# The experts' loop of a hybrid decoder layer: a pair's scatter placed among the next pair's first products, and both experts' first products ahead of the second ones

## The chip, the core and the metric

The kernel runs on one core of a Trainium2 chip. A core has TensorE (PE: matrix products; its weight loads are listed as PEld), VectorE (DVE), ScalarE (ACT), GpSimd (POOL) and SyncE (SP), which here issues the transfers. TensorE's clock has two levels, 1.2 and 2.4 GHz; the profile gives the granted clock as a share of the higher one. The metric is the device time of one execution in microseconds (us), as the median of several runs.

## The reference

One decoder layer is computed for 256 tokens of width 2048: a norm with modulation, a mixer, a residual addition, a second norm, a mixture of experts, a residual addition and a final norm. All values are float32. Only the mixture matters here: each token goes to 2 of 32 experts, and each expert is a gated product of width 512.

```python
def expert_block(args):                       # one expert e, a block of rows xb
    xb, e = args
    hid = jax.nn.silu(xb @ w_gate[e]) * (xb @ w_up[e])     # 2048 -> 512, twice
    return hid @ w_down[e]                                 # 512 -> 2048
...
y = grouped_expert_mlp(xt, eidx, w_gate, w_up, w_down)     # (T, 2, D)
return jnp.einsum('tk,tkd->td', gates.astype(y.dtype), y).reshape(B, S, D)
```

The weights of one expert are 8 + 4 MiB, so the 32 experts bring 384 MiB that are each read once.

## The kernel before

The mixer's part ends at about 680 us; what follows is the experts' loop (`for e in range(0, NE, 2)`), which takes the experts in 16 pairs. Four experts' tokens are gathered at once (`Slots.gather_all`, tiles `xg`, in PSUM bank `g`), so a gather stands at every second pair. For an expert, up to 64 tokens fill the slots.

- `hidden` makes the **first products** (tile `u`, line 1136 and the next): 8 ring tiles of 1 MiB, each with gate and up weights for 256 rows of the input. ScalarE and VectorE then make `hid` (L1140, L1141), TensorE transposes it (L1144, bank `t`), VectorE copies it to `hidT` (L1146).
- `seconds` makes the **second products** (tile `d`): 4 ring tiles of 1 MiB. VectorE scales the result into `z` (L1165), ScalarE rounds it to `yah` or `ybh` (L1168), VectorE forms the rest `yal` or `ybl` (L1169).
- `scatter` brings a finished pair back to the tokens: 8 **blocks** of four products each (`yah`, `yal`, `ybh`, `ybl` with the one-hot matrix `wt`), all of them in the single PSUM bank `s`, each followed by VectorE's addition to the residual tile `xt` (L1182). A block can begin only when the addition of the block before has read the bank.
- `back` makes `wt` and the gates `gs` of a pair, through bank `t` (products `t<-identr,oh` and `t<-Ge,oh`). `further` counts overfull experts, in the first pair only.

All weights go through one ring of slots, 14 of 1 MiB in this loop, which `Stream` hands out in the order of the code: a load is added for each tile (`exp_load`, issued on SP at L191), and it gets the slot of the tile that was used 14 tiles earlier. SP's queue runs in order: a load whose slot is not free yet holds up all loads behind it.

The order within an engine's queue is not that of the code. A scheduler with a timeline of its own sorts the instructions when the kernel is built; waits for slots, banks and tiles decide at run time. L65 is the helper `mm` that records every product. TensorE's products in float32 leave two records each in the trace, so that a ring tile is 8 records of `u` or 16 of `d`.

Of the kernel before, what the change touches and what calls it, by code (L numbers as in the profile page):

```python
# [8 lines left out]
F32 = mybir.dt.float32  # L9
F32R = mybir.dt.float32r  # L10
# [3 lines left out]
ALU = mybir.AluOpType  # L14
AX = mybir.AxisListType

P = 128
D = 2048
NB = 2
KT = 16  # L20
# [9 lines left out]
NE = 32  # L30
# [18 lines left out]
def hybrid_moe(ctx: ExitStack, tc: tile.TileContext, x, c, norm1_g, norm2_g, early, ada_w, ada_b, w_bb,  # L49
# [3 lines left out]
    V, S, G, T = nc.vector, nc.scalar, nc.gpsimd, nc.tensor  # L53
# [10 lines left out]
    def mm(o, lhsT, rhs, start=True, stop=True):  # L64
        return T.matmul(o, lhsT, rhs, start=start, stop=stop, skip_group_check=True)  # L65
# [20 lines left out]
    x1 = x_tiles()  # L86
# [16 lines left out]
    def bank(tag, bufs=None, name=None):  # L103
        return psum.tile([P, 512], F32, name=name or tag, tag=tag, bufs=bufs or BANKS[tag])
# [56 lines left out]
    st = Stream()  # L161
# [28 lines left out]
    def exp_load(w, e, j):  # L190
        return lambda t: nc.sync.dma_start(t, w[e, j])  # L191
# [279 lines left out]
    w_items = [(early_load("out", n, q), None) for qs in ((0, 3), (1, 2)) for n in range(4) for q in qs]  # L471
    for s, load, _ in a_cols + c_cols + z_cols + on(st, w_items) + rows_q:
        s.add(load)
    for e in range(NE):
        for j in range(KT // 2):
            st.add(exp_load(expert_gu, e, j))
        for n in range(4 if e < NE - 2 else 0):
            st.add(exp_load(expert_dn, e, n))

    for n in range(4):  # L480
        for e in (NE - 2, NE - 1):
# [537 lines left out]
    def hid_tile(name):  # L1019
        return cst.tile([P, 4, 4, 40], F32, name=name, tag="rw").rearrange("p n k e -> p (n k e)")[:, 0:512]  # L1020
# [105 lines left out]
                       self.ge[:, b, 2 * a:2 * a + 2], start=(b == 0), stop=(b == 1))  # L1126
            V.tensor_copy(self.gs.rearrange("p h u -> p (h u)"), p[:, 0:4])

    def hidden(u, us, xg, st):
        us = slice(SL * us, SL * (us + 1))  # L1130
        p = bank("u", 2)
        for j in range(KT // 2):
            t = st.get().rearrange("p (k w n) -> p k w n", k=2, w=2)
            for k in range(2):
                kt = 2 * j + k
                mm(p[0:64], xg[:, kt, us], t[:, k, 0], start=(kt == 0), stop=(kt == 15))
                mm(p[64:128], xg[:, kt, us], t[:, k, 1], start=(kt == 0), stop=(kt == 15))
            st.done()
        hid = hid_tile("hid")
        S.activation(hid[64:128], p[0:64], AF.Silu)  # L1140
        V.tensor_tensor(hid[0:64], hid[64:128], p[64:128], op=ALU.mult)  # L1141
        p = bank("t", 1)
        for ft in range(4):
            T.transpose(p[:, SL * ft:SL * (ft + 1)], hid[0:64, P * ft:P * (ft + 1)], ident[0:64, 0:64])  # L1144
        hT = hidT[:, u]
        V.tensor_copy(hT.rearrange("p f s -> p (f s)"), p[:, 0:256])  # L1146
        return hT
# [23 lines left out]
    def seconds(u, hT, gs, ys, st, yl=None):  # L1171
        for n in (0, 2):
            second(u, hT, gs, ys, st, n, 2, yl)

    def scatter(n, wt, yh, yl):
        c = slice(256 * n, 256 * (n + 1))
        for b in range(NB):
            p = bank("s", 1)
            for h in range(2):
                mm(p[:, 256 * h:256 * (h + 1)], wt[:, h, b], yh[h][:, c], start=True, stop=False)  # L1180
                mm(p[:, 256 * h:256 * (h + 1)], wt[:, h, b], yl[h][:, c], start=False, stop=True)
            V.tensor_tensor(x1[n][:, b], x1[n][:, b], p, op=ALU.add)  # L1182

    def scatter_late(n, wt, ys):
        for h, y in enumerate(ys):
            p = bank("g", 2)
            for b in range(NB):
                mm(p[:, 256 * b:256 * (b + 1)], wt[:, h, b].bitcast(F32), y[:, 256 * n:256 * (n + 1)])
            xh = x1[n][:, :, 256 * h:256 * (h + 1)]
            V.tensor_tensor(xh, xh, p.rearrange("p (b j) -> p b j", b=NB), op=ALU.add)  # L1190
# [12 lines left out]
    def new_y(dt, s):  # L1203
        return tuple(mp.tile([P, 1024], dt, name=f"y{h}{s}", tag=f"y{h}{s}", bufs=1) for h in "ab")
# [6 lines left out]
    def further():  # L1211
# [11 lines left out]
        V.tensor_copy(ovi, ove[:, NE - 1:NE])  # L1223
        V.memset(kc, 0.0)

    for e in range(0, NE, 2):
        a = e // 2 % 2
        if not a:
            sl = Slots(Pm[:, :, e:e + 4], Ge[:, :, e:e + 4], 2)
            sl.gather_all()  # L1230
        if e:
            sl.back(a)
        if e == NE - 2:
            hT = [hidden(u, 2 * a + u, sl.xg, st) for u in range(2)]
            break
        hT = hidden(0, 2 * a, sl.xg, st)
        if not e:
            gates()
            sl.back(a)
            further()  # L1240
        yh, yl = new_y(F32R, "h"), new_y(F32R, "l")
        seconds(0, hT, sl.gs, yh, st, yl)
        seconds(1, hidden(1, 2 * a + 1, sl.xg, st), sl.gs, yh, st, yl)
        for n in range(4):
            scatter(n, sl.wt, yh, yl)

    def spare_tile(name, shape):
        pool, tag = slot = next(x for x in st.free if x[0] is not ring1)
# [10 lines left out]
    ys = new_y(F32, "h")  # L1259
    for n in range(4):  # L1260
        for u in range(2):
            second(u, hT[u], sl.gs, ys, st, n, 1)
        scatter_late(n, sl.wt, ys)
        squares(n)
        if n == 0:
            scaled()
            S.activation(small("warm", [P, 1]), ss3[:, 0, 0:1], AF.Sqrt)
# [6 lines left out]
    with tc.For_i(0, nov, 1):  # L1274
        V.tensor_scalar(osel, ovs, kc, None, op0=ALU.is_le)
        V.scalar_tensor_tensor(osel, ove, kc, osel, op0=ALU.is_gt, op1=ALU.mult)
        V.tensor_scalar(oacc, ovs, kc, -float(SL), op0=ALU.subtract, op1=ALU.mult)
        V.scalar_tensor_tensor(oacc, oacc, float(SL), osel, op0=ALU.add, op1=ALU.mult, accum_out=oev[:, 0:1])
        V.scalar_tensor_tensor(oacc, iota32, 0.0, osel, op0=ALU.add, op1=ALU.mult, accum_out=oev[:, 1:2])
        V.tensor_copy(oei, oev[:, 1:2])  # L1280
        ev = nc.sync.value_load(oei[0:1, 0:1], min_val=0, max_val=NE - 1)
        for b in range(NB):
            V.scalar_tensor_tensor(oacc, Pm[:, b], 0.0, osel, op0=ALU.add, op1=ALU.mult, accum_out=opm[:, b, 0:1])
            V.scalar_tensor_tensor(oacc, Ge[:, b], 0.0, osel, op0=ALU.add, op1=ALU.mult, accum_out=opm[:, b, 1:2])
            V.tensor_scalar(opm[:, b, 0:1], opm[:, b, 0:1], oev[:, 0:1], None, op0=ALU.subtract)
        V.tensor_scalar(kc, kc, 1.0, None, op0=ALU.add)
        so = Stream()
        es = bass.ds(ev, 1)

        def dyn(w, j):  # L1290
            return lambda t: nc.sync.dma_start(t, w[es, j].rearrange("e p n -> p (e n)"))

        for w, m in ((expert_gu, KT // 2), (expert_dn, 4)):
            for j in range(m):
                so.add(dyn(w, j))
        so.grow(*main, *side)
        sl = Slots(*(opm[:, :, i:i + 1].to_broadcast([P, NB, 2]) for i in range(2)), 1)
        sl.gather_all()
        sl.back(0)
        ys = new_y(F32, "h")  # L1300
        G.memset(ys[0][64:128], 0.0)
        G.memset(ys[1][0:64], 0.0)
        seconds(0, hidden(0, 0, sl.xg, so), sl.gs, ys, so)
        for n in range(4):
            scatter_late(n, sl.wt, ys)
            squares(n)
        scaled()
# [80 lines left out]
```

## Time and profile before

| | |
|---|---|
| median of 3 runs | 1670.57 us (1669.73 to 1675.09) |
| profiled execution, its own time | 1678.59 us |
| its span, first to last instruction | 1676.8 us |
| mean granted clock of TensorE | 0.962 |
| busy share of the span | PE 93%, DVE 40%, ACT 24%, POOL 11% |
| moved in all | 573.77 MB, 342 GB/s over the span |
| SP's transfers | 85.0% of 16 DMA engines' span |

The profiled execution has a time of its own, above the median, and the durations below are parts of it. A busy share says how much of the span an engine had an instruction in progress, not that it ran at full speed.

### The profile page before, as it was taken

To read this page: it belongs to the slowest core of one execution; us is meant where nothing else is said; L and a number is where in the kernel's file an instruction comes from. 1 tells how busy PE (TensorE), PEld (TensorE's weight loads), DVE (VectorE), ACT (ScalarE), POOL (GpSimd) and SP (SyncE) were. 2 spreads that over 40 slices of the span, in tenths; PEclk is the share of its full clock that TensorE was granted. 3 is DMA by queue.
4 is the path that set the end of the run, shared out by engine and by line. 5 is a ranking of instruction groups with operands and counts; after the bars stand their busy time and mean duration, and the time that the engine had idled before them with its cause. 6 is when DMAs were issued, how large, how long until landed. Compare 5 with 4: busy or idle time off the path is not lost. (4 is left out here: it accounts for less than half of the span.)

```text
span 1676.8 us, 23825 instructions
## 1 busy us (share of the span) xinstructions
PE 1558.4 (93%) x10064; PEld 962.1 (57%) x10064; DVE 670.5 (40%) x1138; ACT 400.8 (24%) x685; POOL 182.5 (11%) x104
## 2 busy tenths in 40 slices
PE   5899899999999999889989889989999999999995
PEld 3678767888877677445444444444444545445443
DVE  3534755234424444343332333333433433434324
ACT  3323654344246344021010011011011011111102
POOL 1111222452223231000000000000000000000000
PEclk8999999999999999899989898999999999999998
DMA  9985467545598784799899798989999999999996
GB/s 391 402 321 225 161 222 282 224 172 203 190 330 334 299 357 160 256 422 420 355 400 421 308 422 353 422 361 420 421 421 421 421 420 420 421 421 420 421 421 231
DMA packets 82438, 573.77 MB, mean 342 GB/s; under 512 B 9740, under 2 KB 10100, under 8 KB 13336
## 3 DMA queue, kind: packets, MB, share of 16 engines
q1 hardware_dynamic: 82080, 572.02, 85.0%
q8 instruction: 81, 1.33, 0.3%
q14 instruction: 29, 0.24, 0.0%
q10 hardware_dynamic: 248, 0.19, 0.0%
HBM read 570.07 MB, written 2.10 MB: 341 GB/s over the span
## 5 line engine op out<-in xcount | busy, mean ns | idle before, releaser
L65 PE MATMUL u<-ring,xg 128*64 128x512 f32 x2048 | 475.6, 599 | 0.0
L65 PEld LDWEIGHTS u<-ring,xg 128*64 128x64 f32 x2048 | 139.8, 137 | 240.0 <-issue 220.1
L65 PE MATMUL d<-ring,hidT 128*64 128x256 f32 x2048 | 250.4, 401 | 9.6 <-DVE hidT L1146 9.6
L65 PE MATMUL w<-hx,stg 128*128 128x256 f32 x1392 | 198.3, 294 | 9.8 <-ACT stg L289 3.1
L65 PEld LDWEIGHTS d<-ring,hidT 128*64 128x64 f32 x2048 | 148.8, 144 | 93.2 <-issue 16.7
L65 PEld LDWEIGHTS w<-hx,stg 128*128 128x128 f32 x1392 | 177.5, 195 | 41.5 <-issue 24.0
L290 POOL TENSOR_TENSOR stg<-ring,stg 128x1024 fp32r<-128x1024 f32 x53 | 128.1, 2417 | 412.4 <-ACT stg L289 370.2
L1182 DVE TENSOR_TENSOR xt<-xt,s 128x512 f32<-128x512 f32 x120 | 82.4, 687 | 225.0 <-PE s L65 224.2
L289 ACT CAST stg<-ring 128x1024 fp32r<-128x1024 f32 x116 | 121.2, 1047 | 187.8 <-PE w L65 150.8
L1165 DVE SCALAR_TENSOR_TENSOR z<-d,gs,g2b 64x512 f32<-64x512 f32 x120 | 90.0, 750 | 166.2 <-PE d L65 164.2
L290 DVE TENSOR_TENSOR stg<-ring,stg 128x1024 fp32r<-128x1024 f32 x63 | 82.1, 1305 | 107.2 <-ACT stg L289 106.4
L65 PE MATMUL prow<-ring,csil 128*32 128x512 f32 (+1 forms) x896 | 113.0, 565 | 0.3 <-DVE csil L180 0.3
L1257 POOL TENSOR_TENSOR xf<-xt,fgb 128x1024 f32<-128x1024 f32 x1 | 2.4, 2362 | 987.0 <-DVE xt L1190 987.0
L1140 ACT ACTIVATE hid<-u 64x512 f32<-64x512 f32 x32 | 18.8, 589 | 333.9 <-PE u L65 330.9
L65 PEld LDWEIGHTS w<-stg,hx 128*128 128x128 f32 x672 | 83.6, 189 | 22.3 <-issue 18.0
L65 PE MATMUL w<-stg,hx 128*128 128x256 f32 (+1 forms) x672 | 96.1, 288 | 0.0
L1168 ACT CAST ybh<-z 64x512 fp32r<-64x512 f32 x60 | 37.0, 617 | 217.2 <-DVE z L1165 215.8
L65 PEld LDWEIGHTS s<-yah,wt 128*128 128x128 f32 x120 | 23.2, 194 | 100.5 <-issue 60.3
L1105 DVE TENSOR_TENSOR xg<-g,sh2c 128x512 f32<-128x512 f32 x64 | 43.4, 688 | 78.8 <-PE u L65 53.2
L65 PE MATMUL g<-oh,h2hi 128*128 128x256 f32 x256 | 68.9, 303 | 6.3 <-DVE xg L1105 5.6
L1168 ACT CAST yah<-z 64x512 fp32r<-64x512 f32 x60 | 37.0, 617 | 156.9 <-DVE z L1165 156.9
L65 PE MATMUL s<-yah,wt 128*128 128x256 f32 x120 | 47.8, 398 | 20.1 <-DVE xt L1182 12.8
(388 smaller groups left out, 1668.7 us busy)
## 6 DMA issues: line engine op xcount, KB each, us to landing
ring<-in_expert_gu_dram SPq DMA_DIRECT2D x256, 1024.0 KB, 13.5
ring<-in_expert_dn_dram SPq DMA_DIRECT2D x128, 1024.0 KB, 14.5
ring<-in_early_dram SPq DMA_DIRECT2D x90, 1024.0 KB, 8.6
ring<-in_ada_w_dram SPq DMA_DIRECT2D x64, 1024.0 KB, 5.3
xt<-in_x_dram SPq DMA_DIRECT2D x8, 512.0 KB, 6.9
out_dram<-xt SPq DMA_DIRECT2D x8, 256.0 KB, 4.5
fgb<-in_final_norm_g_dram SPq DMA_DIRECT2D x1, 1024.0 KB, 21.5
rw<-in_router_w_dram SPq DMA_DIRECT2D x1, 320.0 KB, 5.4
```

Source lines behind the costliest of these rows:

```text
L65: return T.matmul(o, lhsT, rhs, start=start, stop=stop, skip_group_check=True)
L289: S.copy(hi, src)
L290: (G if nsplit[0] % GS[part] == GS[part] - 1 else V).tensor_tensor(lo, src, hi, op=ALU.subtract)
L1105: V.tensor_tensor(self.xg[:, 2 * q:2 * q + 2, 0:w], p[:, 0:2 * w].rearrange("p (k s) -> p k s", k=2), sh2c.rearrange("p n k -> p (n k)")[: ...
L1140: S.activation(hid[64:128], p[0:64], AF.Silu)
L1165: V.scalar_tensor_tensor(o.rearrange("p (n j) -> p n j", n=m), pd[q, 0:256 * m].rearrange("p (n j) -> p n j", n=m), gs[q, h, u:u + 1], g2h ...
L1168: S.copy(ys[h][q, c], o)
L1182: V.tensor_tensor(x1[n][:, b], x1[n][:, b], p, op=ALU.add)
L1257: G.tensor_tensor(xf, x1[0], fgb[:, None, 0:512].to_broadcast([P, NB, 512]), op=ALU.mult)
```

## The change

The loop's body is reordered. `hidden` is split: `turned` now has the transpose. For each pair both experts' first products are written first, then the next gather if one is due, then both transposes and second products. The scatter of a pair is no longer written behind its second products: its 8 blocks are kept in `behind` and are called one after each ring tile of the next pair's first expert. The loads are added in the same order: 16 tiles for the first products of a pair, then 8 for the second ones. `hid` has a tile of its own, and `further` stands behind the first pair. Sizes, banks, slots and the work itself are the same.

```diff
@@ -471,11 +471,13 @@
     w_items = [(early_load("out", n, q), None) for qs in ((0, 3), (1, 2)) for n in range(4) for q in qs]
     for s, load, _ in a_cols + c_cols + z_cols + on(st, w_items) + rows_q:
         s.add(load)
-    for e in range(NE):
-        for j in range(KT // 2):
-            st.add(exp_load(expert_gu, e, j))
-        for n in range(4 if e < NE - 2 else 0):
-            st.add(exp_load(expert_dn, e, n))
+    for e in range(0, NE, 2):
+        for u in range(2):
+            for j in range(KT // 2):
+                st.add(exp_load(expert_gu, e + u, j))
+        for u in range(2 if e < NE - 2 else 0):
+            for n in range(4):
+                st.add(exp_load(expert_dn, e + u, n))
 
     for n in range(4):
         for e in (NE - 2, NE - 1):
@@ -1126,7 +1128,9 @@
                        self.ge[:, b, 2 * a:2 * a + 2], start=(b == 0), stop=(b == 1))
             V.tensor_copy(self.gs.rearrange("p h u -> p (h u)"), p[:, 0:4])
 
-    def hidden(u, us, xg, st):
+    def hidden(us, xg, st, between=()):
+        between = deque(between)
         us = slice(SL * us, SL * (us + 1))
         p = bank("u", 2)
         for j in range(KT // 2):
@@ -1136,9 +1140,14 @@
                 mm(p[0:64], xg[:, kt, us], t[:, k, 0], start=(kt == 0), stop=(kt == 15))
                 mm(p[64:128], xg[:, kt, us], t[:, k, 1], start=(kt == 0), stop=(kt == 15))
             st.done()
-        hid = hid_tile("hid")
+            if between:
+                between.popleft()()
+        hid = mp.tile([P, 512], F32, name="hid", bufs=1)
         S.activation(hid[64:128], p[0:64], AF.Silu)
         V.tensor_tensor(hid[0:64], hid[64:128], p[64:128], op=ALU.mult)
+        return hid
+    def turned(u, hid):
         p = bank("t", 1)
         for ft in range(4):
             T.transpose(p[:, SL * ft:SL * (ft + 1)], hid[0:64, P * ft:P * (ft + 1)], ident[0:64, 0:64])
@@ -1172,14 +1181,13 @@
         for n in (0, 2):
             second(u, hT, gs, ys, st, n, 2, yl)
 
-    def scatter(n, wt, yh, yl):
+    def scatter(n, b, wt, yh, yl):
         c = slice(256 * n, 256 * (n + 1))
-        for b in range(NB):
-            p = bank("s", 1)
-            for h in range(2):
-                mm(p[:, 256 * h:256 * (h + 1)], wt[:, h, b], yh[h][:, c], start=True, stop=False)
-                mm(p[:, 256 * h:256 * (h + 1)], wt[:, h, b], yl[h][:, c], start=False, stop=True)
-            V.tensor_tensor(x1[n][:, b], x1[n][:, b], p, op=ALU.add)
+        p = bank("s", 1)
+        for h in range(2):
+            mm(p[:, 256 * h:256 * (h + 1)], wt[:, h, b], yh[h][:, c], start=True, stop=False)
+            mm(p[:, 256 * h:256 * (h + 1)], wt[:, h, b], yl[h][:, c], start=False, stop=True)
+        V.tensor_tensor(x1[n][:, b], x1[n][:, b], p, op=ALU.add)
 
     def scatter_late(n, wt, ys):
         for h, y in enumerate(ys):
@@ -1223,26 +1231,33 @@
         V.tensor_copy(ovi, ove[:, NE - 1:NE])
         V.memset(kc, 0.0)
 
+    sl = Slots(Pm[:, :, 0:4], Ge[:, :, 0:4], 2)
+    sl.gather_all()
+    behind = []
     for e in range(0, NE, 2):
         a = e // 2 % 2
-        if not a:
-            sl = Slots(Pm[:, :, e:e + 4], Ge[:, :, e:e + 4], 2)
-            sl.gather_all()
-        if e:
-            sl.back(a)
-        if e == NE - 2:
-            hT = [hidden(u, 2 * a + u, sl.xg, st) for u in range(2)]
-            break
-        hT = hidden(0, 2 * a, sl.xg, st)
+        now = sl
+        hid = [hidden(2 * a, now.xg, st, behind)]
         if not e:
             gates()
-            sl.back(a)
+        now.back(a)
+        wt, gs = now.wt, now.gs
+        hT = [turned(0, hid[0])] if e == NE - 2 else []
+        hid.append(hidden(2 * a + 1, now.xg, st))
+        if a and e < NE - 2:
+            sl = Slots(Pm[:, :, e + 2:e + 6], Ge[:, :, e + 2:e + 6], 2)
+            sl.gather_all()
+        if e == NE - 2:
+            hT.append(turned(1, hid[1]))
+            break
+        yh, yl = new_y(F32R, "h"), new_y(F32R, "l")
+        for u in range(2):
+            seconds(u, turned(u, hid[u]), gs, yh, st, yl)
+        behind = [lambda n=n, b=b, a=(wt, yh, yl): scatter(n, b, *a) for n in range(4) for b in range(NB)]
+        if not e:
             further()
-        yh, yl = new_y(F32R, "h"), new_y(F32R, "l")
-        seconds(0, hT, sl.gs, yh, st, yl)
-        seconds(1, hidden(1, 2 * a + 1, sl.xg, st), sl.gs, yh, st, yl)
-        for n in range(4):
-            scatter(n, sl.wt, yh, yl)
 
     def spare_tile(name, shape):
         pool, tag = slot = next(x for x in st.free if x[0] is not ring1)
@@ -1259,8 +1274,8 @@
     ys = new_y(F32, "h")
     for n in range(4):
         for u in range(2):
-            second(u, hT[u], sl.gs, ys, st, n, 1)
-        scatter_late(n, sl.wt, ys)
+            second(u, hT[u], gs, ys, st, n, 1)
+        scatter_late(n, wt, ys)
         squares(n)
         if n == 0:
             scaled()
@@ -1300,7 +1315,7 @@
         ys = new_y(F32, "h")
         G.memset(ys[0][64:128], 0.0)
         G.memset(ys[1][0:64], 0.0)
-        seconds(0, hidden(0, 0, sl.xg, so), sl.gs, ys, so)
+        seconds(0, turned(0, hidden(0, sl.xg, so)), sl.gs, ys, so)
         for n in range(4):
             scatter_late(n, sl.wt, ys)
             squares(n)
```

What the scheduler made of it is shown at three places. Names are those above; "x16" counts the program's products of one kind in a row (4 of `u` or 8 of `d` are a ring tile).

TensorE's queue where the second pair ends and the third begins. Before, four blocks of the scatter stand in a row, of which the last one is shown, ahead of two ring tiles of second products:

```order
L65 MATMUL s<-yah,wt 128x256
L65 MATMUL s<-yal,wt 128x256
L65 MATMUL s<-ybh,wt 128x256
L65 MATMUL s<-ybl,wt 128x256
L65 MATMUL d<-ring,hidT 64x256 x16
L65 MATMUL u<-ring,xg 64x512 x17
L65 MATMUL s<-yah,wt 128x256
L65 MATMUL u<-ring,xg 64x512
L65 MATMUL s<-yal,wt 128x256
L65 MATMUL s<-ybh,wt 128x256
L65 MATMUL s<-ybl,wt 128x256
L65 MATMUL u<-ring,xg 64x512 x14
```

The same place after the change:

```order
L65 MATMUL d<-ring,hidT 64x256 x4
L1153 MATMUL t<-ident,hid 128x64 x4
L65 MATMUL u<-ring,xg 64x512 x4
L65 MATMUL d<-ring,hidT 64x256 x32
L65 MATMUL u<-ring,xg 64x512 x5
L65 MATMUL s<-yah,wt 128x256
L65 MATMUL u<-ring,xg 64x512 x3
L65 MATMUL s<-yal,wt 128x256
L65 MATMUL s<-ybh,wt 128x256
L65 MATMUL s<-ybl,wt 128x256
L65 MATMUL u<-ring,xg 64x512 x4
L65 MATMUL t<-identr,oh 128x128
```

The blocks moved behind all second products and in between the first products of the next pair, one tile of which (`u` x4) stands ahead of the last 4 tiles of second products.

TensorE's queue in a later pair without a gather, before the change, from the gates to the scatter's beginning:

```order
L65 MATMUL t<-Ge,oh 128x2 x4
L1144 MATMUL t<-ident,hid 128x64 x4
L65 MATMUL d<-ring,hidT 64x256 x32
L65 MATMUL u<-ring,xg 64x512 x32
L1144 MATMUL t<-ident,hid 128x64 x4
L65 MATMUL d<-ring,hidT 64x256 x8
L65 MATMUL t<-identr,oh 128x128 x4
L65 MATMUL d<-ring,hidT 64x256 x16
L65 MATMUL s<-yah,wt 128x256
L65 MATMUL d<-ring,hidT 64x256 x8
L65 MATMUL s<-yal,wt 128x256
```

And after it:

```order
L65 MATMUL u<-ring,xg 64x512 x4
L65 MATMUL t<-Ge,oh 128x2 x4
L65 MATMUL u<-ring,xg 64x512 x4
L1153 MATMUL t<-ident,hid 128x64 x4
L65 MATMUL u<-ring,xg 64x512 x28
L65 MATMUL d<-ring,hidT 64x256 x8
L1153 MATMUL t<-ident,hid 128x64 x4
L65 MATMUL t<-identr,oh 128x128 x4
L65 MATMUL d<-ring,hidT 64x256 x48
L65 MATMUL s<-yah,wt 128x256
L65 MATMUL s<-yal,wt 128x256
L65 MATMUL s<-ybh,wt 128x256
```

The first expert's transpose (`t<-ident,hid`) and the gates moved in among first products, and the second expert's transpose stands behind a tile of second products.

SP's queue, the first loads of experts, before:

```order
L191 DMA ring<-in_expert_gu_dram 128x2048 x7
L191 DMA ring<-in_expert_dn_dram 128x2048 x4
L191 DMA ring<-in_expert_gu_dram 128x2048 x9
L191 DMA ring<-in_expert_dn_dram 128x2048
L191 DMA ring<-in_expert_gu_dram 128x2048 x2
L191 DMA ring<-in_expert_dn_dram 128x2048
L191 DMA ring<-in_expert_gu_dram 128x2048 x3
L191 DMA ring<-in_expert_dn_dram 128x2048 x4
L191 DMA ring<-in_expert_gu_dram 128x2048 x2
L191 DMA ring<-in_expert_dn_dram 128x2048 x2
```

And after:

```order
L191 DMA ring<-in_expert_gu_dram 128x2048 x14
L191 DMA ring<-in_expert_dn_dram 128x2048
L191 DMA ring<-in_expert_gu_dram 128x2048
L191 DMA ring<-in_expert_dn_dram 128x2048 x6
L191 DMA ring<-in_expert_gu_dram 128x2048
L191 DMA ring<-in_expert_dn_dram 128x2048
L191 DMA ring<-in_expert_gu_dram 128x2048 x11
L191 DMA ring<-in_expert_dn_dram 128x2048 x2
L191 DMA ring<-in_expert_gu_dram 128x2048 x4
L191 DMA ring<-in_expert_dn_dram 128x2048 x6
```

The first pair's 16 tiles of first products are now loaded almost at once, and from the third pair on the loads alternate 16 and 8 (before: 8 and 4, with the two kinds mixed for the first pairs).

## Rows read from the trace of the kernel before

**Rows 1.** The page: span, and the granted clock in 40 slices

```profile
span 1676.8 us, 23825 instructions
...
PEclk8999999999999999899989898999999999999998
```

**Rows 2.** Busy time by stage: stretch, length, engines, then clock, DMA share, GB/s

```profile
680.00:720.00 40.00, 40.00 (x192) 19.27 (x192) 6.81 (x11) 1.88 (x3) 0.00 (x0) 0.96 0.75 281
720.00:800.00 80.00, 75.30 (x478) 40.54 (x475) 35.88 (x77) 15.51 (x24) 0.00 (x0) 0.96 1.01 421
800.00:1114.00 314.00, 284.94 (x1611) 145.34 (x1611) 108.23 (x167) 31.77 (x53) 0.00 (x0) 0.92 0.92 377
1114.00:1620.00 506.00, 481.53 (x2922) 238.58 (x2920) 190.60 (x294) 56.81 (x94) 0.00 (x0) 0.99 1.01 421
1620.00:1652.00 32.00, 30.85 (x190) 15.28 (x188) 10.31 (x20) 4.52 (x9) 0.00 (x0) 1.00 0.99 412
```

**Rows 3.** The first dip of the transfers, by the same columns

```profile
800.00:810.00 10.00, 7.37 (x45) 5.78 (x45) 6.11 (x10) 0.21 (x1) 0.00 (x0) 0.80 0.87 359
810.00:820.00 10.00, 10.00 (x56) 4.43 (x54) 2.87 (x4) 1.23 (x2) 0.00 (x0) 0.86 0.61 226
```

**Rows 4.** Waits of SP's queue, 795 to 815 us: total, times, longest

```profile
SPq L191 <- PE d L65: 20.8, 4, 13.9
```

**Rows 5.** Timeline of TensorE there: start, length, group, idle before it

```profile
794.31 3.67 PE L65 MATMUL d<-ring,hidT 128*64 128x256 f32 x32
...
804.16 0.40 PE L65 MATMUL s<-yah,wt 128*128 128x256 f32 x1 [1.07 <-DVE xt L1182]
...
805.69 0.39 PE L65 MATMUL s<-yah,wt 128*128 128x256 f32 x1 [0.78 <-DVE xt L1182]
...
807.47 0.58 PE L65 MATMUL s<-yah,wt 128*128 128x256 f32 x1 [0.78 <-DVE xt L1182]
...
808.62 5.72 PE L65 MATMUL d<-ring,hidT 128*64 128x256 f32 x32
```

**Rows 6.** Timeline of TensorE: gates of pairs 1, 14, 15, 16; first products of an expert

```profile
726.58 1.05 PE L65 MATMUL t<-Ge,oh 128*128 128x2 f32 x8
...
1505.45 1.05 PE L65 MATMUL t<-Ge,oh 128*128 128x2 f32 x8
...
1566.87 1.05 PE L65 MATMUL t<-Ge,oh 128*128 128x2 f32 x8 [0.69 <-ACT wt L1119]
...
1576.10 13.90 PE L65 MATMUL u<-ring,xg 128*64 128x512 f32 x64
...
1621.53 1.05 PE L65 MATMUL t<-Ge,oh 128*128 128x2 f32 x8
```

**Rows 7.** Waits of TensorE, 1140 to 1620 us: total, times, longest

```profile
PE t L1144 <- DVE hid L1141: 5.9, 4, 1.5
...
PE t L1144 <- DVE gs L1127: 3.7, 8, 0.7
...
PE t L65 <- ACT wt L1119: 2.7, 4, 0.7
```

**Rows 8.** Waits of TensorE's weight loads for a transfer, 720 to 1140 us

```profile
PEld u L65 <- DMA ring<-in_expert_gu_dram: 0.9, 3, 0.3
...
PEld d L65 <- DMA ring<-in_expert_dn_dram: 0.2, 1, 0.2
```

**Rows 9.** Timeline of TensorE in the first pair

```profile
734.43 0.69 PE L1144 MATMUL t<-ident,hid 64*128 64x64 f32 x4 [3.93 <-DVE ovn L1217]
735.64 6.37 PE L65 MATMUL d<-ring,hidT 128*64 128x256 f32 x32 [0.52 <-DVE hidT L1146]
```

**Rows 10.** The end: last expert loads on SP, and the last second products

```profile
1616.06 17.75 SPq L191 DMA_DIRECT2D ring<-in_expert_dn_dram  x8
...
1656.86 1.95 PE L65 MATMUL d<-ring,hidT 128*64 128x256 f32 x16
```

**Rows 11.** Loads of 1140 to 1620 us: count, size, median us to landing

```profile
ring<-in_expert_dn_dram SPq DMA_DIRECT2D x62, 1024.0 KB, 18.4
```

## The prediction, made before the changed kernel ran

> **What bounds the kernel now.** I read the page first, for the granted clock over the span: its low digits lie in the first half of the experts' loop, and its second half stands at 9 throughout but for the last slice [rows 1]. Then the table by stage, to see which resource is full where. From 720 to 800 us and again from 1114 to 1620 us the transfers run at 421 GB/s with a share of 1.01; they cannot go faster. Between, from 800 to 1114 us, they fall to 377 GB/s, and there the clock is 0.92 instead of 0.99 [rows 2]. All bytes after 720 us are weights that must come in any case, so what the transfers lose in the middle is never regained. The loss is 314 us x (1 - 377/421) = **32.8 us**.
>
> Why they pause is seen at the first dip, 800 to 820 us, where they fall to 359 and then 226 GB/s [rows 3]. SP's queue stood still for up to 13.9 us, until second products had released a ring slot [rows 4]. TensorE was late with those: it first went through four blocks of the scatter in a row, each waiting 0.78 to 1.07 us for VectorE to empty bank `s`. Half idle in this way it lost its clock (0.80 and 0.86 in these two slices, so part of the time at the lower of its two levels, 1.2 GHz), and the next two ring tiles of second products took 5.72 us, against 3.67 us for two such tiles just before [rows 3, 5]. So it is a chain: scatter in a row, waits, low clock, late slots, idle transfers.
>
> The other side is TensorE's own time. It waits for a transfer for only about 1 us in 420 [rows 8]; every microsecond of its chain counts too. The gates of a pair mark its progress. From pair 1 to pair 16 it takes 1621.53 - 726.58 = 894.95 us. The last two intervals are 61.42 us (with a gather) and 54.66 us (without) [rows 6]. Fifteen intervals like these, 7 with and 8 without, would take 867.2 us: the early pairs cost TensorE 27.7 us more than the late ones. Both bounds show nearly the same surplus in the same stretch.
>
> **The change, part by part.** *The scatter between first products.* The late pairs do this already before the change: the scheduler put the blocks there by itself, one per ring tile, where the tile's products hide VectorE's addition. What is new is that the early pairs do it too. In the order after the change no block of the scatter stands ahead of second products that SP waits for, except in late pairs one or two ahead of a pair's last tile. Two rows of blocks remain: four between the first and second pair's products, three between the second's and third's. I count 3 + 2 waits of 0.78 us = 3.9 us, and for the clock twice the excess of the slow tiles, 5.72 - 3.67 = 2.05 us, so 4.1 us [rows 5]: 8.0 us of new cost for TensorE. It gets back the 27.7 us of the early pairs.
>
> *Both experts' first products ahead.* The wait for `hid` before its transpose (5.9 us in 1140 to 1620 us), for the gates' copy (3.7 us) and for `wt` (2.7 us) now lie behind a tile of products: 12.3 us in four double pairs, 3.1 us each [rows 7]. Over 7.5 double pairs that is 23.1 us.
>
> *`further` behind the first pair.* It held bank `t` ahead of the second expert's transpose for 3.93 us, and two slow tiles followed at 6.37 us [rows 9]. The transfers ran at their full rate meanwhile [rows 2]; it only adds to TensorE's arrears before the first dip. I take nothing for it, and at most 3.93 + 6.37 - 3.67 = 6.6 us.
>
> *The order of the loads* now is the order of use. Its danger is at the start: 14 slots now hold first products only, and one tile of the second pair's first products is the 24th load but is used ahead of the first second products. The 24th load waits for the tenth used tile. The 6 tiles used after that keep TensorE 6 x 1.74 = 10.4 us (an expert's 8 tiles take 13.90 us [rows 6]), and a load takes 1.049 MB / 421 GB/s = 2.49 us [rows 2], so up to three others may be ahead of it and it still lands in time. Cost nothing; if it is late, once, by the length of a few loads, under 8 us, and the transfers run meanwhile.
>
> *The longest stretch without a released slot* is what decides whether transfers pause. In the new order it is some blocks of scatter or half a gather, 4 to 6 us; the old one had 13.9 us [rows 4].
>
> **The sum.** TensorE: 27.7 + 23.1 - 8.0 = 42.8 us less. The transfers allow 32.8 us, and a little more at the end: the last expert load is issued by 1633.8 us and lands about 18.4 us later, near 1652.2 us, and its products begin at 1656.86 us [rows 10, 11]. These 4.7 us are TensorE's arrears, which it can make up. Floor of the transfers: 37.5 us. The smaller of the two limits counts, 37.5 us. I leave 3.5 us of it for one pause at the early rows of scatter (the first dip of before is worth 10 x (1 - 359/421) + 10 x (1 - 226/421) = 6.1 us, and I take somewhat over half) [rows 3]. That is **34 us** of the profiled execution's 1678.59 us. This execution is 8.0 us above the median. The work of two executions is the same, so the 8 us are waits or lost clock somewhere; no row says where. I put half of them into the very pauses that go away, and expect 30 us at the median: 1670.57 - 30 = **1640.6 us**. Likely in this case: 1629 to 1648 us.
>
> **Rivals.** *Half of it.* The pauses hang on 14 slots and on a queue in order; an early pair that still falls behind by some tiles keeps some of its dips. The old kernel has them up to 1114 us although single causes are small, which speaks for a slow recovery; against it, TensorE's pair becomes shorter than its loads: (61.42 + 54.66 - 3.1) / 2 = 56.5 us against 24 x 2.49 = 59.8 us. If half of the 32.8 us stay, 16 us are gained: 1654 us (1648 to 1665).
>
> *It does nothing.* The late pairs before had this order, more or less, and if the early pauses come from something else in those pairs (the gathers, the arrears from the mixer's end with 281 GB/s from 680 to 720 us [rows 2]) the transfers lose the same as ever: 1665 to 1676 us. The dip's chain speaks against it, since it names the blocks and the second products [rows 4, 5].
>
> *Slower: TensorE runs ahead and loses its clock.* When it has caught up it must wait for each tile of first products, 2.49 - 1.74 = 0.75 us. The rows show that waits of 0.78 us between short products are enough to lose the clock [rows 3, 5]. If that happens in all pairs, the slack of 3.3 us per pair decides: slow tiles cost 5.72 - 3.67 = 2.05 us per two, so from about four slow tiles per pair on TensorE is the bound and the transfers pause everywhere. At the 377 GB/s of the disturbed stretch, the bytes of 1114 to 1652 us (506 x 421 + 32 x 412 = 226 MB, in us x GB/s) take 600 us instead of 538: 62 us longer, near 1733 us. Against it: a TensorE that falls behind has full work again, and in the late stretch the clock is 0.99 with 4 to 5% of idle time [rows 2]. The Trainium skill, "TensorE: Matmul & The Clock Gate", section "HAM oscillation — how this bites in real kernels", tells of just this: a product loop whose work is shorter than its wait for weights loses the clock at each tile, and the advice is to keep products together. By it the scatter among first products is the better order and a TensorE ahead of its loads the worse one; no row of this trace shows waits for a transfer long enough to tell.
>
> **How the numbers follow.** Chances: the pauses go, 0.62; half of it, 0.20; nothing, 0.09; slower, 0.09. About 0.3%, 5 us, is what a measurement of this kernel can tell from no change. So faster 0.82, same 0.09, slower 0.09. The range reaches from the floor, 1670.57 - 37.5 - 5 = 1628 us, over the second case up to 1662 us; that holds nearly all of the first case and most of the second, about 0.8.
>
> **What would show it.** Right: 421 GB/s from 720 us to the last expert load; a clock near 1.0 from the third pair on; VectorE's additions to `xt` no longer ahead of TensorE in its waits; SP waiting for transfers and first products more than for second ones; gates 55 to 60 us apart from the start. Wrong: dips of the transfers after 830 us; waits of TensorE for transfers together with a clock under 0.95; gates over 60 us apart on average; or an end that comes well behind the last load's landing.

## The result, and the profile after

The changed kernel takes **1647.14 us** (median of 4 runs, 1645.27 to 1648.37) against 1670.67 us beside it: ratio 0.9849, 95% interval 0.9834 to 0.9864. A second measurement, of 5 runs against 15 of the kernel before (1668.62 to 1679.44), gave 1644.53 us against 1674.47 us: 0.9819 (0.9797 to 0.9841). The forecast was 1640.6 us, 1628 to 1662. In the profiled executions the span went from 1676.8 to 1643.4 us, by 33.4 us, where 34 was forecast.

Page of the changed kernel, part 2: granted clock and bytes moved in 40 slices.

```profile
PEclk8999999999999999799999999999999999999998
GB/s 392 408 329 237 162 206 293 246 155 161 225 309 315 308 369 178 232 397 421 420 419 421 421 420 421 421 420 420 421 420 421 420 421 421 421 421 421 420 420 218
```

The table by stage of the same execution, the counterpart of [rows 2], ends each row with granted clock, share of the DMA engines and GB/s:

```profile
680.00:720.00 40.00, 40.00 (x194) 19.38 (x192) 8.06 (x21) 4.15 (x6) 0.00 (x0) 0.96 0.78 303
720.00:800.00 80.00, 77.05 (x477) 41.62 (x478) 35.72 (x68) 11.05 (x17) 0.00 (x0) 0.96 1.01 420
800.00:1114.00 314.00, 305.32 (x1838) 149.35 (x1836) 122.02 (x188) 37.16 (x61) 0.00 (x0) 0.99 1.01 420
1114.00:1590.00 476.00, 454.25 (x2730) 219.82 (x2726) 178.71 (x274) 53.61 (x88) 0.00 (x0) 1.00 1.01 421
```

The 377 GB/s of 800 to 1114 us have become 420. The last expert load says what that is worth. SP's timeline at the end, and TensorE's last second products (start, duration, instruction):

```profile
1583.28 17.74 SPq L191 DMA_DIRECT2D ring<-in_expert_dn_dram  x8
```

```profile
1623.79 1.95 PE L65 MATMUL d<-ring,hidT 128*64 128x256 f32 x16
```

The last load is issued by 1583.28 + 17.74 = 1601.0 us, against 1633.8 us [rows 10]: 32.8 us earlier, the loss worked out in the prediction. (That it agrees to the tenth is chance: 420 instead of 421 GB/s still loses 0.7 us, and 303 instead of 281 GB/s from 680 to 720 us give a lead of 2 us.) The last products start 33.1 us earlier (1656.86 before [rows 10]). Both ends moved together.

SP's longest waits (us in total, times, longest): for second products before the change, from 720 to 1140 us; then those after it, from 720 to 1140 us and from 1140 to 1590 us:

```profile
SPq L191 <- PE d L65: 176.7, 56, 14.1
```

```profile
SPq L191 <- PE u L65: 172.3, 90, 7.3
SPq L191 <- PE d L65: 99.4, 49, 6.1
```

```profile
SPq L191 <- DMA ring<-in_expert_gu_dram: 261.7, 123, 3.2
SPq L191 <- DMA ring<-in_expert_dn_dram: 117.4, 56, 2.1
SPq L191 <- PE u L65: 7.6, 28, 0.4
```

The longest wait for second products is down from 14.1 us (13.9 us at the first dip [rows 4]) to 6.1 us. In the second stretch SP waits for transfers, not for TensorE: slots are ready before the bytes have come. TensorE meets the same bound, in its waits from 1140 to 1590 us and in its timeline at the end (in brackets the wait before the instruction and what ended it):

```profile
PE d L65 <- DMA ring<-in_expert_dn_dram: 7.8, 15, 0.7
PE u L65 <- DMA ring<-in_expert_gu_dram: 5.0, 11, 0.6
PE s L65 <- ACT yah L1177: 2.8, 5, 0.6
PE g L65 <- DVE xg L1107: 2.4, 3, 0.8
```

```profile
1588.23 1.94 PE L65 MATMUL u<-ring,xg 128*64 128x512 f32 x8 [0.20 <-DMA ring<-in_expert_gu_dram]
1590.72 1.94 PE L65 MATMUL u<-ring,xg 128*64 128x512 f32 x8 [0.55 <-DMA ring<-in_expert_gu_dram]
```

The waits for `hid`, `gs` and `wt` [rows 7] are gone; those for loads are new. A ring tile now takes 0.55 + 1.94 = 2.49 us, the time of its load. TensorE's timeline at the gates, to be read against [rows 6], shows when it got there:

```profile
719.19 1.05 PE L65 MATMUL t<-Ge,oh 128*128 128x2 f32 x8
...
1057.53 1.05 PE L65 MATMUL t<-Ge,oh 128*128 128x2 f32 x8
...
1108.36 1.05 PE L65 MATMUL t<-Ge,oh 128*128 128x2 f32 x8
...
1171.78 1.05 PE L65 MATMUL t<-Ge,oh 128*128 128x2 f32 x8
...
1286.03 1.05 PE L65 MATMUL t<-Ge,oh 128*128 128x2 f32 x8
...
1406.39 1.05 PE L65 MATMUL t<-Ge,oh 128*128 128x2 f32 x8
...
1581.13 1.05 PE L65 MATMUL t<-Ge,oh 128*128 128x2 f32 x8
```

Up to 1286 us no wait of TensorE is one for a load. There it needs 50.8 us for a pair and 63.4 us for one with a gather, 114.2 us for two. From 1286 us on two pairs take it 120.4 us, about the 48 x 2.49 = 119.5 us of the transfers. The whole way from pair 1 to pair 16 takes 861.94 us instead of 894.95.

### The profile page after: what moved, and what is told of

Same layout as the page of the kernel before. It is cut to its first block, busy times and chain, and to the rows that moved or that the text cites. A ratio compares the mean times of both kernels' runs of the same rounds, so it can differ in the third digit from the quotient of the medians.

```text
span 1643.4 us, 23829 instructions
## 1 busy us (share of the span) xinstructions
PE 1545.9 (94%) x10064; PEld 945.0 (58%) x10064; DVE 672.1 (41%) x1138; ACT 398.6 (24%) x683; POOL 182.8 (11%) x104
## 5 line engine op out<-in xcount | busy, mean ns | idle before, releaser
L65 PE MATMUL u<-ring,xg 128*64 128x512 f32 x2048 | 485.9, 604 | 7.8 <-DMA ring<-in_expert_gu_dram 7.8
L65 PEld LDWEIGHTS u<-ring,xg 128*64 128x64 f32 x2048 | 134.3, 137 | 236.1 <-issue 190.5
L65 PE MATMUL d<-ring,hidT 128*64 128x256 f32 x2048 | 238.1, 382 | 10.5 <-DMA ring<-in_expert_dn_dram 8.9
L65 PEld LDWEIGHTS d<-ring,hidT 128*64 128x64 f32 x2048 | 144.0, 137 | 90.9 <-issue 10.3
L1147 DVE TENSOR_TENSOR hid<-hid,u 64x512 f32<-64x512 f32 x32 | 22.1, 690 | 134.0 <-ACT hid L1146 133.8
L1121 ACT CAST wt<-t 128x512 fp32r<-128x512 f32 x16 | 9.4, 587 | 233.7 <-PE s L65 222.6
## 6 DMA issues: line engine op xcount, KB each, us to landing
ring<-in_expert_gu_dram SPq DMA_DIRECT2D x256, 1024.0 KB, 19.8
ring<-in_expert_dn_dram SPq DMA_DIRECT2D x128, 1024.0 KB, 19.8
fgb<-in_final_norm_g_dram SPq DMA_DIRECT2D x1, 1024.0 KB, 19.8
```

What stands on the lines that cost most here:

```text
L1121: S.copy(self.wt.rearrange("p h b t -> p (h b t)"), p)
```

## Experiments

**Which half of the change does it.** e1_first keeps both experts' first products ahead and the new order of the loads, and writes the scatter behind the second products again:

```diff
-        hid = [hidden(2 * a, now.xg, st, behind)]
+        hid = [hidden(2 * a, now.xg, st)]
...
-        behind = [lambda n=n, b=b, a=(wt, yh, yl): scatter(n, b, *a) for n in range(4) for b in range(NB)]
+        for n in range(4):
+            for b in range(NB):
+                scatter(n, b, wt, yh, yl)
```

> The scatter is written behind a pair's second products again; both experts' first products ahead, the order of the loads and the rest stay as in the changed kernel. In this order the scheduler puts the blocks of the scatter between the next pair's first products by itself. Theory (the place in the code does not matter, the order of first products and loads brings it): 1647 us, within 3 us, transfers at 421 GB/s throughout from 720 us. Rival (the deferred scatter carries the gain): pauses come back, 1655 to 1670 us.

1642.34 us (1639.63 to 1646.12), 0.9812 (0.9788 to 0.9837) of the kernel before; 421 GB/s from 800 to 1590 us. Nothing came back. In its trace TensorE's products and SP's loads stand in the same order as in that of the changed kernel. As it lay somewhat under the changed kernel, both were measured again side by side:

> The changed kernel once more, beside the one with the scatter written behind the second products. Theory (both give the same queues on TensorE and SP, and what differs between executions is only how much has been loaded ahead of 720 us): 1643 to 1648 us, within 0.3% of the other; a profiled execution that ends earlier has moved more from 680 to 720 us, by 40 us x (difference of the rates) / 421. Rival (the place of the scatter in the code costs something): the other is faster by 3 us or more again.

> The scatter written behind the second products, once more, beside the changed kernel on the same chip. Theory: the same time as the changed kernel within 0.3%. Rival: faster by 3 us or more.

1644.53 and 1644.72 us: the same. The rival falls. The two profiled executions, 1644.8 and 1637.6 us long, moved 294 and 365 GB/s from 680 to 720 us: 40 x (365 - 294) / 421 = 6.7 us, near the 7.2 us between them, as expected. The other way round, e2_scatter keeps the deferred scatter and restores the old order of experts and loads:

```diff
+    for e in range(NE):
+        for j in range(KT // 2):
+            st.add(exp_load(expert_gu, e, j))
+        for n in range(4 if e < NE - 2 else 0):
+            st.add(exp_load(expert_dn, e, n))
...
-        hT = [turned(0, hid[0])] if e == NE - 2 else []
+        hT = [turned(0, hid[0])]
+        if e < NE - 2:
+            yh, yl = new_y(F32R, "h"), new_y(F32R, "l")
+            seconds(0, hT[0], gs, yh, st, yl)
```

> The other half alone: the scatter is called between the next pair's first products, but an expert's second products again stand ahead of the next expert's first ones, and loads come as 8 and 4. In its order rows of four blocks still stand ahead of second products in the second to fourth pair, and only from about the sixth pair on one block follows each tile. Theory (rows of blocks, and a queue of loads held by second products, make the pauses): a part of them comes back, 1655 to 1668 us, with dips of the transfers before 1000 us and SP waiting for second products by over 10 us at once. Rival (deferring the scatter is the whole gain): 1647 us.

1672.70 us (1666.25 to 1675.76), 0.9993 (0.9977 to 1.0008): no gain clear of noise, somewhat worse than expected. Its stages from 800 to 1590 us, and its longest waits of SP from 760 to 1114 us:

```profile
800.00:1114.00 314.00, 285.99 (x1655) 143.63 (x1654) 108.79 (x167) 33.37 (x55) 0.00 (x0) 0.95 0.97 396
1114.00:1590.00 476.00, 454.90 (x2717) 227.01 (x2716) 179.53 (x276) 53.58 (x88) 0.00 (x0) 0.97 1.01 420
```

```profile
SPq L191 <- PE u L65: 150.3, 89, 5.2
SPq L191 <- PE d L65: 147.8, 45, 13.2
```

The pauses are there again, with 13.2 us at once, but they are smaller: 314 x (1 - 396/421) = 18.6 us instead of 32.8. That even this gains nothing is TensorE's doing. From the gates of pair 1 (719.30 us) to those of pair 16 (1617.24 us) it takes 897.9 us, no less than the 894.95 before; the last load is issued 11.0 us earlier than before (by 1622.8 us), but the last second products start only 4.3 us earlier (1652.57 us). No row of blocks is left from 965 to 1590 us, and still the clock is 0.97 from 1114 us. It falls there six times, each time at waits around a transpose and the gates beside it (`wt`, `gs`, `hid`, `hidT`), most of which the first products ahead take away. TensorE's timeline at one of them:

```profile
1228.03 0.46 PE L1151 MATMUL t<-ident,hid 64*128 64x64 f32 x4 [1.47 <-DVE hid L1145]
1229.01 3.58 PE L65 MATMUL d<-ring,hidT 128*64 128x256 f32 x16 [0.52 <-DVE hidT L1153]
```

The tile takes 3.58 us instead of 1.95. So the first products ahead do two things, which no run parts: the early blocks find room among first products, and the waits around the transposes go. Nor is the order of the loads parted from that of the products; the slots are handed out in one order for both. The other edits (`hid` in a tile of its own, `further` behind the first pair, the deferred scatter) are all in e2_scatter and by themselves gain nothing.

**How much margin TensorE has.** e3_light leaves the low parts' products out, e9_heavy1 and e10_heavy2 do them two and three times; behind the third pair the order is otherwise that of the changed kernel (in e3_light but for the place of the gates). The edit for three times:

```diff
-                mm(p[:, 256 * h:256 * (h + 1)], wt[:, h, b], yl[h][:, c], start=False, stop=True)
+            for k in range(3):
+                mm(p[:, 256 * h:256 * (h + 1)], wt[:, h, b], yl[h][:, c], start=False, stop=k == 2)
```

> The changed kernel without the scatter's products of the low parts: the low halves of the experts' results are left out of the sum. TensorE has about 1.9 us less to do per pair, 28 us in 15 pairs. Theory (the transfers are the bound from 720 us on, TensorE has a surplus of 5 us per double pair): 1647 us, within 3 us; more waits for transfers, clock still 0.98 or more. Rival 1 (TensorE is the bound): 1620 to 1625 us. Rival 2 (a TensorE that runs ahead of its loads loses its clock at each tile): clock under 0.95 behind 1114 us and over 1655 us.

> The changed kernel with the scatter's products of the low parts done twice in each block, so that the low halves count double in the sum. The order behind the third pair is the same. Two more products of 0.12 us in each of 8 blocks are 1.9 us per pair, 28.8 us in the 15 intervals between the gates of pair 1 and pair 16. Theory: TensorE's own pace there is 846 us (566.8 us up to 1286.03 us, then 3 x 50.8 + 2 x 63.4 us), the transfers held it to 861.9 us; 16 us of margin are used up, and the time grows by 28.8 - 16 = 13 us against the changed kernel, to 1655 to 1662 us. Rival 1 (the transfers leave more room): no change. Rival 2 (there is no room, each product counts): 29 us more, 1672 to 1678 us.

> The same with the low parts' products done three times, 3.84 us per pair, 57.6 us in 15 intervals. Theory: 57.6 - 16 = 42 us more than the changed kernel, 1684 to 1691 us, slower than the kernel before, with the clock at 0.98 or more and transfers under 421 GB/s. Rival 1: no change up to 1650 us. Rival 2: 58 us more, over 1700 us.

| low parts' products | none | once (changed kernel) | twice | three times |
|---|---|---|---|---|
| time, us | 1645.76 | 1647.14, 1644.53 | 1646.31 | 1670.75 |
| ratio to before | 0.9833 | 0.9849, 0.9819 | 0.9836 | 0.9992 |

Flat, flat, flat, then a step: the transfers set the time until TensorE's pace passes theirs. Three times, at the gates of pairs 9, 11 and 16, and the last second products:

```profile
1197.39 1.05 PE L65 MATMUL t<-Ge,oh 128*128 128x2 f32 x8
...
1319.21 1.05 PE L65 MATMUL t<-Ge,oh 128*128 128x2 f32 x8
...
1617.45 1.05 PE L65 MATMUL t<-Ge,oh 128*128 128x2 f32 x8
...
1654.49 1.95 PE L65 MATMUL d<-ring,hidT 128*64 128x256 f32 x16
```

121.8 us for two pairs, 7.6 more than 114.2 as expected, and above the 119.5 us of the loads. The clock is 1.00 and the transfers run at 413 GB/s from 1114 to 1590 us, as expected. But the end moved by 30.7 us, not 42, and twice the products cost about nothing instead of 13. The margin was counted only up to pair 16's gates, 16 us. From there to the last products the changed kernel takes 42.66 us (1623.79 - 1581.13) and this one 37.04 us: 5.6 us more of margin lay in the last pair, which also waits for its loads. That makes a margin of 21.5 us. The 30.7 us of three times are no test of it, as the 5.6 us were read from the same run (its way between the gates is 898.2 us). Twice is one: its way is 870.1 us against TensorE's own 846.0 us, so 870.1 - 846.0 - 21.5 = 2.6 us should be left over, and its profiled execution takes 962.7 us from its first products to the end, against 960.0 us.

In e3_light, TensorE waits longest for loads (from 1140 to 1590 us):

```profile
PE u L65 <- DMA ring<-in_expert_gu_dram: 17.7, 32, 1.6
PE d L65 <- DMA ring<-in_expert_dn_dram: 10.4, 20, 0.7
```

Its clock is 1.00 from 1114 to 1590 us all the same. Ahead of that stretch stands a longer wait, and there it is not. TensorE's timeline:

```profile
1068.23 7.04 PE L65 MATMUL d<-ring,hidT 128*64 128x256 f32 x48 [2.14 <-DMA ring<-in_expert_dn_dram]
```

The granted clock is 0.57 from 1068 to 1072 us, and these three tiles take 7.04 us, where two at the higher level take 3.67 us. In this trace it happened this once.

**Fewer bytes.** e4_bytes brings half of each second-products tile:

```diff
+        return lambda t: nc.sync.dma_start(t[:, 0:1024], w[e, j, :, 0:1024])
...
-                st.add(exp_load(expert_dn, e + u, n))
+                st.add(exp_half(expert_dn, e + u, n))
...
-                    mm(pd[64 * v:64 * (v + 1), 256 * n:256 * (n + 1)], hT[:, ft], t[:, ft, o:o + 256],
+                    mm(pd[64 * v:64 * (v + 1), 256 * n:256 * (n + 1)], hT[:, ft], t[:, ft % 2 if yl else ft, o:o + 256],
```

> The changed kernel, but of each ring tile for second products in the first 30 experts only one half is loaded and used twice, so these products have wrong weights and all of their number. The transfers of a double pair take 99.6 instead of 119.6 us, TensorE's work is the same. Theory (TensorE's own pace is 114.2 us per double pair, just under the transfers' pace): TensorE becomes the bound, the stretches of 120 us per double pair become 114, and the time falls by only 10 to 18 us, to 1629 to 1637 us. Rival (TensorE has much room left, its pace was only that of the loads): up to 62.9 MB less at 421 GB/s, 149 us: 1500 to 1600 us.

1692.34 us, 1.0126 (1.0090 to 1.0161): with 63 MB less to move the kernel is slower than before the change. Both theories missed, because the queue has another order, presumably as the scheduler reckons with shorter loads: a row of up to five blocks in front of second products in each double pair. So it does not test TensorE's margin, but it gives the price of such a row. TensorE's timeline at one of them:

```profile
1263.53 0.36 PE L65 MATMUL s<-yah,wt 128*128 128x256 f32 x1 [0.87 <-DVE xt L1193]
...
1265.02 0.39 PE L65 MATMUL s<-yah,wt 128*128 128x256 f32 x1 [0.78 <-DVE xt L1193]
1265.24 0.28 PE L65 MATMUL s<-yal,wt 128*128 128x256 f32 x1
1265.36 0.28 PE L65 MATMUL s<-ybh,wt 128*128 128x256 f32 x1
...
1268.91 0.41 PE L65 MATMUL s<-yal,wt 128*128 128x256 f32 x1
1269.13 0.41 PE L65 MATMUL s<-ybh,wt 128*128 128x256 f32 x1
```

Waits of 0.78 us stand between blocks of about as much work, and within the row the products' spacing goes from 0.12 to 0.22 us: the lower clock level. Its stage and its longest wait of SP, both from 1114 to 1590 us:

```profile
1114.00:1590.00 476.00, 455.76 (x2590) 231.21 (x2588) 172.02 (x263) 49.56 (x82) 0.00 (x0) 0.95 0.86 340
```

```profile
SPq L194 <- PE d L65: 171.2, 59, 16.9
```

From pair 3 on two pairs take 122.8 to 126.7 us, where the same products take 114.2 us in the changed kernel.

**Without the wait for VectorE.** e6_bank is the kernel before with two banks for the blocks:

```diff
-            p = bank("s", 1)
+            p = bank("s", 1) if b else bank("g", 2)
```

> The kernel before, but the scatter's blocks use bank s and the gather's bank g in turn, so that a block need not wait until VectorE has read the block before. Its order is another one: four blocks ahead of second products in all pairs, and the gathers at the start of a double pair. Theory (a row of blocks costs by its waits, and by the clock that TensorE loses in them): TensorE keeps its clock, 0.98 or more in the loop, and the pauses shrink, 1648 to 1662 us; what is left are pauses where SP's queue stands behind second products. Rival 1 (not the waits in the row but its place ahead of second products makes the pauses): dips in all pairs, 1670 to 1700 us, the clock near 1.0 all the same. Rival 2 (nothing to do with the blocks): 1670 us.

1702.86 us, 1.0190 (1.0159 to 1.0221): the theory missed, the first rival was right on the time (a little over its range) but not on the clock, which is 0.95. The edit does what it should: TensorE's waits for VectorE's addition, before the change

```profile
PE s L65 <- DVE xt L1182: 12.8, 16, 1.1
```

from 720 to 1140 us, are 0.7 us from 720 to 1114 us. But another wait stands in their place, and now in the late pairs too, which had none for the addition. From 1114 to 1590 us:

```profile
PE g L65 <- ACT yah L1168: 24.0, 15, 2.3
```

The blocks now stand right behind the second products whose result they need, and wait for ScalarE's rounding of it. So the wait for VectorE was not tested apart from the place of the blocks; how much of the 32 us is the new wait and how much the other changes of this order is not separated.

**Another execution of before.**

> The kernel before once more, to see another execution of it. Theory (the profiled execution stood 8 us above the median because its pauses were longer): an execution near 1670 us has the same gates' intervals behind 1114 us and a smaller loss of the transfers from 800 to 1114 us, about 25 instead of 32.8 us. Rival (the 8 us are spread over the span, in the mixer as well): the loss in 800 to 1114 us stays 30 to 35 us and the stages ahead of 680 us are shorter.

It took 1674.29 us, with a span of 1672.5 us and 381 GB/s from 800 to 1114 us, a loss of 29.8 us, and 419 GB/s up to 1590 us, another 2.3 us: close to the rival's 30 to 35 us, and not 25. The first products behind the mixer, in the timelines of the first profile of before, of e5_before, of the changed kernel, of e7_after and of e8_first:

```profile
683.95 3.65 PE L65 MATMUL u<-ring,xg 128*64 128x512 f32 x16
```

```profile
677.05 3.65 PE L65 MATMUL u<-ring,xg 128*64 128x512 f32 x16
```

```profile
683.37 3.65 PE L65 MATMUL u<-ring,xg 128*64 128x512 f32 x16
```

```profile
684.50 3.65 PE L65 MATMUL u<-ring,xg 128*64 128x512 f32 x16
```

```profile
677.15 3.65 PE L65 MATMUL u<-ring,xg 128*64 128x512 f32 x16
```

The loop starts up to 7 us earlier or later with the same queues (those of e7_after and e8_first are the same, too). From there to the end of the span it is 992.9 and 995.5 us before the change (spans 1676.8 and 1672.5), and 960.0, 960.3 and 960.5 us (spans 1643.4, 1644.8, 1637.6) after it. The change is worth 32 to 36 us from there on, whichever of these are compared; a late start of the loop is added to that.

## Why the prediction was right, step by step

**The two bounds.** Right. The transfers' loss of 32.8 us came back but for 0.7 us, and they are the bound now. TensorE's own way is 846.0 us (566.8 up to 1286.03 us, then 3 x 50.8 + 2 x 63.4): 48.9 us shorter, where 42.8 was forecast. Its parts were mis-sized: seven pairs with a gather and eight without, at 63.4 and 50.8 us, are 850.2 instead of 867.2 us, so hiding the waits gave 17.0 us, not 23.1; the other 31.9 us are the early pairs, for which 27.7 - 8.0 was put. As the transfers were the smaller limit, none of this reached the end.

**The scatter between first products.** Right on what costs time, wrong on what brings it. The prediction split the gain between the scatter's new place and the first products ahead. e1_first and e2_scatter show that the first products ahead, with the loads in their order, do all of it, and the deferred scatter alone nothing. And the rows are not all that costs TensorE its clock: e2_scatter loses it in late pairs without a row. The two early rows of blocks are there, at about the forecast price. TensorE's timeline of the changed kernel at the first, the like of [rows 5]:

```profile
762.98 0.58 PE L65 MATMUL s<-yah,wt 128*128 128x256 f32 x1 [0.78 <-DVE xt L1190]
...
764.14 3.68 PE L65 MATMUL u<-ring,xg 128*64 128x512 f32 x8
```

In the stretch from 720 to 1140 us the waits for `xt` are 4.0 us (3.9 forecast), in total still the most of TensorE's waits there, though the prediction's signs of being right had it otherwise. The tile behind this row takes 3.68 us instead of 1.94, the one behind the other row 3.58: 3.4 us (4.1 forecast).

**The 3.5 us for a pause, the 4.7 us of arrears.** Both off, and it is luck that they nearly cancelled: 34 forecast, 33.1 measured at the last products. No pause was left, and the 4.7 us were no arrears. TensorE's first second products of the last pair, before and after the change:

```profile
1636.83 1.90 PE L65 MATMUL d<-ring,hidT 128*64 128x256 f32 x16
```

```profile
1603.72 1.95 PE L65 MATMUL d<-ring,hidT 128*64 128x256 f32 x16 [1.11 <-DMA ring<-in_expert_dn_dram]
```

After the change this tile waits for its load, and stands 20.44 us behind the issue of the last eight loads (1583.28); before, it stood 20.77 us behind it (1616.06 [rows 10]). So TensorE's arrears were 0.3 us. From this tile to the last one it takes 20.0 us before and 20.1 us after, without a wait for a load: that is its own time for the last tiles and the blocks between them, which no earlier load shortens. The floor of the transfers was 33.1 us and not 37.5.

**The 24th load and `further`.** Right: the tile behind the first gates starts without a wait, and transfers run at 420 GB/s from 720 us.

**From the profile to the median.** "I put half of them into the very pauses that go away" is the step that failed in its reason. e5_before ended 4.3 us earlier than the first profile of before; it began the loop 6.9 us earlier and took 2.6 us more in it. What differs thus lies ahead of the loop and not in its pauses. The profiled execution of before stood 8.0 us above its median, that of the changed kernel 1.9 us below: 33.3 us between the two, 23.5 us between the medians, and 29.9 us in the second measurement, against the 30 of the forecast. Presumably it depends on how often the loop starts late among few runs; where it starts is known of profiled executions alone. The forecast of 1640.6 us is thus 4 to 6.5 us low, under the spread of one kernel's runs.

**The rivals.** Half of it and nothing: no dips are left. A TensorE ahead of its loads that loses its clock: it did come to wait for each tile, by 0.55 us and in e3_light by up to 1.6 us from 1140 us on, and the clock stayed at 1.00. The Trainium skill, "TensorE: Matmul & The Clock Gate", section "HAM oscillation — how this bites in real kernels", speaks of tiles whose products take less time than the wait; here 1.94 us of products stand against these waits, so its condition is not met. Where it was met, once in e3_light with a wait of 2.14 us behind a tile of 1.95 us, the trace agrees: the clock fell. The rows of blocks come near it, with waits of 0.78 us against 0.75 us of products.

## What to carry to other kernels

Where a scheduler orders the queues, look at the order and not at where a line is written: the same order came from two texts, and a smaller load gave another, slower one. When one side of a loop becomes the bound, measure the other's margin by adding work in steps, and count the margin to the end of the last tile. Before a profile is set against a median, find where two executions of the same kernel part: a spread that arises ahead of the change is not the change's to win.

## What the runs showed of the hardware

- One core kept 420 to 421 GB/s for 870 us, from 720 to 1590 us. A load for first products landed a median of 13.9 us after its issue up to 1140 us, and 19.8 us from there on, where SP waited for transfers and not for slots. That is the time of about eight loads of 2.49 us: they queue behind each other, and at the same rate that costs nothing.
- Waits of 0.78 to 0.87 us between blocks of some 0.75 us took the clock to its lower level after two or three of them, with no longer gap in between; so did one wait of 2.14 us behind a tile of 1.95 us (e3_light), and waits of 1.47 and 0.52 us before and behind a transpose (e2_scatter). Waits of 0.55 us between tiles of 1.94 us did not.
- The same queues reach the experts' loop at 677 to 684.5 us in different executions.
